# Down's first weight sums and slots placed anew, three pools of banks, and feed forward's first transposes ahead of the mixer's last row

## The chip, the cores and the metric

The kernel runs on one core of a Trainium2 chip. The metric is device time in microseconds. The engines are TensorE (PE; its weight loads are PEld), VectorE (DVE), ScalarE (ACT), GpSimd (POOL) and SyncE (SP), which issues the DMA transfers. Each engine works through its own list of instructions in order and waits on semaphores for the others.

## The reference

A block of two layers works on 1024 tokens of width 1024, in fp32. Layer 0's mixer joins a short convolution with attention over the 256 best keys; layer 1's is a gated delta rule. The two layers are:

```python
for i in range(2):
    hn = rmsnorm(h, norm_mix_g[i])
    h = h + (conv_dsa_mixer(hn, ...) if i == 0 else gated_deltanet_mixer(hn, ...))
    h = h + swiglu(rmsnorm(h, norm_ffn_g[i]), ffn_w_gate[i], ffn_w_up[i], ffn_w_down[i])
    e = rmsnorm(p[i] @ ple_w_proj[i], ple_post_norm_g[i])
    h = h + e * sigmoid(rmsnorm(h, ple_norm_g[i]) @ ple_w_gate[i])
```

The feed forward's width is 2816, and swiglu(n) is (silu(n @ w_gate) * (n @ w_up)) @ w_down.

## The kernel before

For l = 0 and 1 it runs mixer, feed forward (ffn), embedding stage (ple). A matrix operand in fp32 is split into a high and a low part (split: the high part is a copy on ACT, the low one a subtraction on DVE), and a product is three matmuls, high x high, high x low and low x high.

The feed forward multiplies 2 x 2 blocks with seven products instead of eight. So it needs sums of blocks: POOL makes those of the weights (wino: four sums of 128 x 512; S for gate/up, T_dn for down), those of the normed tokens (T1 to T4) and those of g (Sg). The blocks of tokens, B11, B21, B22 and T1 to T4, are transposed on TensorE (put, tp_f tiles) into H tiles. Gate/up (ffn_gu) goes through 22 groups of 128 hidden columns, two to a pair j: a group adds its seven products into three PSUM banks, pga, pgb and pgc, which ACT and DVE evacuate into g (gate) or u (up). After a pair, DVE multiplies u into g, POOL makes Sg, and SP stores both into a DRAM tile gfD.

Down (ffn_down) goes through 11 pairs in four units of 2, 3, 3 and 3 pairs, with seven steps in each. A step loads its block out of gfD into a slot (x), copies it (y on ACT), leaves the rest in x (DVE), splits its weights into the slot's other half (wh, wl), and multiplies into four banks, pda or pdb by turns; the banks are added into h. Slots are places in SBUF: pools s0 and s7, one tile s12 cut into pieces, and for step 3 the norm's buffers and s3. SBUF pools of the earlier stages are reused, so that a slot is free only when its former user is done.

Of the eight PSUM banks, gate/up uses pga 2, pgb/pgc 2 and the transposes 4, all in one pool, and down pda 4 and pdb 4, in one pool. The attention before has a pool of its own for mm (pswob) and one for its small tiles (tpy, y, tpp).

The order of the instructions comes from a scheduler that walks through the program with estimated times; self.after(marks) makes it issue what follows only after the instructions in marks. In layer 0 the attention's last row ends with finish (y is scaled into yR on DVE, transposed as tpy on TensorE, split, and multiplied by the output weights, pswob) and norm, and only then does the feed forward begin:

```python
            finish(*late)
            norm(NT - 1)
        self.gnes.close()
```

The feed forward's first group has the weights of group 0 behind the attention's last transposed probabilities:

```python
            with self.after(None if l else [self.last_pT]):
                w1, w2 = weights(0)
```

## Time and profile before

| | us |
|---|---|
| median of 3 runs | 2976.1 |
| lowest, highest | 2974.38, 2976.13 |
| profiled execution | 2976.15 |
| its span | 2974.3 |
| busy in it: PE, DVE, ACT, POOL | 2867.7, 1867.2, 1259.4, 1060.5 |

Times below are microseconds from the start of that span. Layer 0's mixer ends at about 689, its gate/up at 1130, its down at 1354; layer 1's mixer ends at 2206, its gate/up at 2650. In a row of the timeline stand the start, the length, the engine, the line, the operation with output and inputs, the shapes, the count, and in brackets the idle time before it and what ended it. Names are cut of their numbers. A row with a count covers several instructions and the gaps between them that the profile shows as none. In a row of waits stand the waiting and the awaited operation, the time in total, how often, and the longest.

### The profile page before, as it was taken

The numbers are of one execution on the slowest core, as the hardware profiler recorded it, in microseconds if no ns is written. First come the engines' busy times: TensorE is split into PE (matmuls) and PEld (weight loads), VectorE is DVE, ScalarE is ACT, GpSimd is POOL, SyncE is SP. The second block draws the span as 40 slices with busy tenths as digits, with TensorE's granted clock in tenths as the row PEclk, the third lists the DMA queues.
The fourth block names the chain that finished last, engine by engine and source line by source line (L and its number), as shares of the span: only waits on it lengthen the run. The fifth ranks groups of instructions, "written<-read, shape, count | busy, mean of one in ns | idle before, by whom it ended". The sixth has DMA issues, their size and how long they took to land.

```text
span 2974.3 us, 47842 instructions
## 1 busy us (share of the span) xinstructions
PE 2867.7 (96%) x19211; PEld 2388.5 (80%) x19211; DVE 1867.2 (63%) x3274; ACT 1259.4 (42%) x2226; POOL 1060.5 (36%) x931
## 2 busy tenths in 40 slices
PE   7999998999999998999999999999999999999999
PEld 6989876797888886888887777788678888878887
DVE  5799995455444448885466767664445444479871
ACT  4467725544333335434445455443233333344341
POOL 1341000114544436435212443342144455556333
PEclk9999998999999999999999999999999999999999
DMA  4122165201322225534332232223711322245422
GB/s 146 50 51 93 57 191 201 90 30 38 112 106 95 103 107 216 190 108 139 107 127 97 94 111 97 87 94 110 266 64 71 113 102 95 105 172 206 162 87 92
DMA packets 119822, 340.80 MB, mean 115 GB/s; under 512 B 11696, under 2 KB 34608, under 8 KB 101936
## 3 DMA queue, kind: packets, MB, share of 16 engines
q1 hardware_dynamic: 119600, 337.74, 32.9%
q8 instruction: 151, 2.47, 0.3%
q14 instruction: 71, 0.58, 0.1%
HBM read 240.64 MB, written 97.06 MB: 114 GB/s over the span
## 4 chain that ended last, share of the span: by engine, by line
PE 83%; DVE 8%; DMA 3%; ACT 3%; issue 2%; POOL 1%; SPq 0%; DVEq 0%; ACTq 0%; POOLq 0%
PE pga L852 16%; PE pgb L852 8%; PE pso L1369 7%; PE pdb L1027 6%; PE pda L1027 6%; PE psp L1138 6%; PE psz L216 4%; PE pgc L852 4%; PE pskqv L227 3%; PE psow L237 3%; PE psz L1629 2%; PE y L743 2%; PE pswob L237 2%; DVE sc L467 1%; PE tpp L734 1%
## 5 line engine op out<-in xcount | busy, mean ns | idle before, releaser
L1027 PE MATMUL pda<-sl 128*128 128x512 f32 x912 | 217.5, 396 | 12.4 <-DVE sl L109 12.3
L1027 PEld LDWEIGHTS pda<-sl 128*128 128x128 f32 x912 | 173.9, 191 | 51.7 <-DVE sl L109 15.4
L1027 PE MATMUL pdb<-sl 128*128 128x512 f32 x888 | 207.9, 391 | 5.4 <-DVE g L937 3.7
L782 POOL TENSOR_TENSOR S<-wr_gu 128x512 f32<-128x512 f32 x44 | 68.8, 1563 | 395.9 <-DMA wr_gu<-in_w_gu_dram 373.8
L1027 PEld LDWEIGHTS pdb<-sl 128*128 128x128 f32 x888 | 167.1, 189 | 41.9 <-DVE g L937 4.1
L109 DVE TENSOR_TENSOR w2l_gu<-S,w2h_gu 128x1024 fp32r<-128x1024 f32 x44 | 67.2, 1528 | 164.4 <-ACT w2h_gu L108 164.3
L1369 PE MATMUL pso<-hh,wl_od 128*128 128x512 f32 x384 | 157.3, 410 | 0.0
L1369 PE MATMUL pso<-hh,wh_od 128*128 128x512 f32 x384 | 156.9, 409 | 0.0
L1369 PE MATMUL pso<-hl,wh_od 128*128 128x512 f32 x384 | 156.4, 407 | 0.0
L1016 ACT CAST sl<-sl 128x1536 fp32r<-128x1536 f32 (+1 forms) x54 | 74.8, 1386 | 145.8 <-DMA sl<-gfD 143.1
L108 ACT CAST w2h_gu<-S 128x1024 fp32r<-128x1024 f32 x44 | 46.3, 1052 | 186.1 <-PE pga L852 94.1
L1387 DVE SCALAR_TENSOR_TENSOR c<-pso,odcw,c 128x509 f32<-128x509 f32 (+1 forms) x144 | 107.0, 743 | 26.5 <-ACT c L1384 24.9
L1017 DVE TENSOR_TENSOR sl<-sl 128x1536 fp32r<-128x1536 f32 (+1 forms) x54 | 103.3, 1914 | 24.7 <-ACT sl L1016 24.5
L227 PE MATMUL pskqv<-wh_kqv,hh 128*128 128x256 f32 x384 | 109.4, 285 | 0.3 <-ACT wh_kqv L108 0.3
L227 PE MATMUL pskqv<-wh_kqv,hl 128*128 128x256 f32 x384 | 108.7, 283 | 0.0
L227 PE MATMUL pskqv<-wl_kqv,hh 128*128 128x256 f32 x384 | 108.3, 283 | 0.0
L603 DVE TENSOR_SCALAR_CACHE_REDUCE tk_junk<-sc,tk_f 128x1024 int8<-128x1024 f32 (+5 forms) x111 | 102.5, 924 | 1.8
L153 POOL TENSOR_SCALAR nss_f<-nss_f 128x1 f32<-128x1 f32 x16 | 3.2, 200 | 273.2 <-ACT junk_f L152 273.2
L1138 PE MATMUL psp<-wh_pg,hh_p 128*128 128x512 f32 x256 | 100.5, 393 | 0.0
L1138 PE MATMUL psp<-wh_pg,hl_p 128*128 128x512 f32 x256 | 99.7, 390 | 0.0
L1138 PE MATMUL psp<-wl_pg,hh_p 128*128 128x512 f32 x256 | 99.7, 389 | 0.0
L600 ACT ACTIVATE tk_junka<-sc,tk_f 128x512 int8<-128x512 f32 (+2 forms) x93 | 83.7, 900 | 34.5 <-DVE tk_f L618 30.3
(543 smaller groups left out, 9013.3 us busy)
## 6 DMA issues: line engine op xcount, KB each, us to landing
wr_gu<-in_w_gu_dram SPq DMA_DIRECT2D x44, 1024.0 KB
sl<-gfD SPq DMA_DIRECT2D x42, 768.0 KB
gfD<-Sg SPq DMA_DIRECT2D x22, 1024.0 KB
wr_dn<-in_w_dn_dram SPq DMA_DIRECT2D x22, 1024.0 KB
wr_od<-in_w_qkv_dram SPq DMA_DIRECT2D x12, 1024.0 KB
...
```

What stands on the lines that cost most here:

```text
L216: nc.tensor.matmul(ps[:M, f * 512:(f + 1) * 512], a[:, kc, c], b[f][:, kc, :], start=(kc == 0 and i == 0), stop=(kc == KC - 1 and i == 2))
L227: nc.tensor.matmul(out, a[:, kc, c], b[:, kc, :], start=(kc == 0 and i == 0), stop=(kc == KC - 1 and i == 2))
L237: nc.tensor.matmul(ps[:, f * 512:(f + 1) * 512], a[:, kc, tsl], b[:, f * 512:(f + 1) * 512], start=(kc == 0 and i == 0), stop=(kc == nk - ...
L600: nc.scalar.activation(jk[:, :n], sc[b], AF.Sign, bias=fb, scale=-1.0, accum_out=c)
L603: v.tensor_scalar(jk[:, :n], sc[b], fb, 0.0, op0=op, op1=ALU.add, accum_out=c)
L852: nc.tensor.matmul(bank, a[:, kc, :], b[:, kc, :], start=first and kc == 0 and m == 0, stop=kc == 3 and m == 2, skip_group_check=True)
L1016: nc.scalar.copy(y, x.bitcast(F32))
L1017: v.tensor_tensor(x, x.bitcast(F32), y.bitcast(F32), op=ALU.subtract)
L1027: nc.tensor.matmul(ps, a[:, i, c], b[:, i, :], start=first and i == 0 and k == 0, stop=i == m - 1 and k == 2, skip_group_check=True)
L1138: nc.tensor.matmul(ps, a[:, kc, c], b, start=kc == 0 and i == 0, stop=kc == KC - 1 and i == 2)
L1369: nc.tensor.matmul(ps[:, f * 512:(f + 1) * 512], a[:, kc, :], b[f][:, kc, :], start=(kc == 0 and i == 0), stop=(kc == KC - 1 and i == 2))
L1387: nc.vector.scalar_tensor_tensor(c[:, e:(f + 1) * 512], ps[:, e - d:(f + 1) * 512 - d], cw[:, k:k + 1], c[:, e:(f + 1) * 512], op0=ALU.mul ...
```

## The change

1. A stage's banks lie in one pool for each tag (a, b, t) instead of one pool for all.
2. The last row's finish is cut in two. The scaling, tpy and the split stay where they are; pswob, the addition and the row norm (last_row) are issued in the feed forward's first group, behind the transposes of B11 and B21 in layer 0 and ahead of them in layer 1. Group 0's weights stand behind the last yR, and group 1's behind the last T sum.
3. The last pair's store to gfD is issued behind the loads of down's unit 0. T_dn of unit 1 stands behind the last Sg. The slots are cut anew, and a step's splits stand behind the splits of the step before and, from unit 1 on, behind the evacuation of three steps ago.
4. In the embedding stage the gate's first weights lie in four pools instead of one.

```diff
     def psum(self, es, name, **tags):
-        self.pss = self.pool(es, name, space=PSUM)
+        self.pss = {t: self.pool(es, name + t, space=PSUM) for t in tags}
...
     def tp(self, name, tag="tp"):
-        return self.pss.tile([P, 512], F32, tag=tag, bufs=self.tags[tag], name=name)
+        return self.pss[tag].tile([P, 512], F32, tag=tag, bufs=self.tags[tag], name=name)
...
                 ps = self.mm(f"pswob{i}")
-                self.mm_R2(ps, (yh, yl), slice(0, P), lambda k: [x[:, k % 2, :] for x in ws[k // 2]], 4)
-                row = self.row_home(i)
-                v.tensor_tensor(row, ps, row, op=ALU.add)
-                nc.sync.dma_start(self.hB[i * P:(i + 1) * P, :], row)
+                def out():
+                    self.mm_R2(ps, (yh, yl), slice(0, P), lambda k: [x[:, k % 2, :] for x in ws[k // 2]], 4)
+                    row = self.row_home(i)
+                    v.tensor_tensor(row, ps, row, op=ALU.add)
+                    nc.sync.dma_start(self.hB[i * P:(i + 1) * P, :], row)
+                return out
...
-            finish(*late)
-            norm(NT - 1)
-        self.gnes.close()
+            self.last_row = (finish(*late), junk(NT - 1))
...
         def group(n, x):
-            w1, w2 = weights(n)
+            with self.after([self.last_T] if n == 1 else None):
+                w1, w2 = weights(n)
...
         def first_group(x):
             hn = self.hn
-            with self.after(None if l else [self.last_pT]):
+            out, junk = self.last_row
+            with self.after(None if l else [self.last_yR]):
                 w1, w2 = weights(0)
+            def last_row():
+                out()
+                self.row_norm(NT - 1, junk)
+                self.gnes.close()
+            if l:
+                last_row()
...
             put("B21", lambda p: hn[2 * p][:, 512:])
+            if not l:
+                last_row()
...
-            nc.sync.dma_start(gD[j, :, 0:2, :], g[:, :, 0, :])
-            nc.sync.dma_start(gD[j, :, 2, :], g[:, 1, 1, :])
-            nc.sync.dma_start(gD[j, :, 3:7, :], S)
+            def store(j=j, g=g, S=S):
+                nc.sync.dma_start(gD[j, :, 0:2, :], g[:, :, 0, :])
+                nc.sync.dma_start(gD[j, :, 2, :], g[:, 1, 1, :])
+                nc.sync.dma_start(gD[j, :, 3:7, :], S)
+            if j < NFF // 2 - 1:
+                store()
+        return store
...
-        slots = itertools.chain((s0, 0, 2, None, 4, s0, 0), (s7, 3, s0, 0) * 3 + (s7, 3), (s0, 0, 3, s0, 0, 3, 0))
+        n0, n7, a, c = new(s0), new(s7), run(sa), cut((sb, 0, 0), (sb, 0, 1), (sa, 6144, None), (s3, 0, 0))
+        slots = itertools.chain((n0, a, run(sa, 4096), own, run(sb), n0, a), (c, n7, n0, a) * 3 + (c, n7), (n0, a, c, n0, a, n0, a))
...
-                self.wino(gp, [T[:, i] for i in range(4)], [q[:, i] for i in range(4)], "right")
+                with self.after([self.last_Sg] if ui == 1 else None):
+                    self.wino(gp, [T[:, i] for i in range(4)], [q[:, i] for i in range(4)], "right")
...
+                if (ui, si) == (0, 6):
+                    with self.after([get]):
+                        store()
...
-                with self.after([self.last_sum] if ui == 0 and si else None):
+                with self.after(prep + evac[:1] if ui else [self.last_sum] if si else None):
...
-            self.pad(es, 17, f"plp0{l}")
-            w0 = mk("w0")
+            self.pad(es, 1, f"plp0{l}")
+            w0 = [mk("w0a")]
+            self.pad(es, 16, f"plp1{l}")
+            w0 += [mk("w0b")] * 3
```

In the pieces below, names are cut of their layer and carry the buffer's number behind; where a line has moved, L852 is now L853, L885 is L896, L1027 is L1050 and L780 is L781. On TensorE, at layer 0's way into the feed forward, before:

```order
L681 MATMUL tpy_6461<-cf,yR_6457 128x128 x4
L237 MATMUL pswob_6468<-wh_wob_4566,yh_6459 128x512 x2
L237 MATMUL pswob_6468<-wl_wob_4567,yh_6459 128x512 x2
...
L237 MATMUL pswob_6468<-wh_wob_4587,yl_6460 128x512 x2
L885 MATMUL tp_f_B_6577<-cf,hn_f_0_4451 128x128 x4
L885 MATMUL tp_f_B_6584<-cf,hn_f_2_4453 128x128 x4
L885 MATMUL tp_f_B_6591<-cf,hn_f_4_4455 128x128 x4
L885 MATMUL tp_f_B_6598<-cf,hn_f_6_4457 128x128 x4
L885 MATMUL tp_f_B_6605<-cf,hn_f_0_4451 128x128 x4
L852 MATMUL pga_0_6574<-HB11h_6525,w1h_gu_0_6562 128x512
L885 MATMUL tp_f_B_6612<-cf,hn_f_2_4453 128x128 x4
```

Now:

```order
L681 MATMUL tpy_6468<-cf,yR_6464 128x128 x4
L237 MATMUL pswob_6475<-wh_wob_4573,yh_6466 128x512 x2
L237 MATMUL pswob_6475<-wl_wob_4574,yh_6466 128x512 x2
L896 MATMUL tp_f_B_6560<-cf,hn_f_0_4458 128x128 x4
L896 MATMUL tp_f_B_6567<-cf,hn_f_2_4460 128x128 x4
L896 MATMUL tp_f_B_6574<-cf,hn_f_4_4462 128x128 x4
L896 MATMUL tp_f_B_6581<-cf,hn_f_6_4464 128x128 x4
L237 MATMUL pswob_6475<-wh_wob_4573,yl_6467 128x512 x2
L237 MATMUL pswob_6475<-wh_wob_4573,yh_6466 128x512 x2
...
L237 MATMUL pswob_6475<-wh_wob_4594,yl_6467 128x512 x2
L896 MATMUL tp_f_B_6588<-cf,hn_f_0_4458 128x128 x4
...
L853 MATMUL pga_0_6557<-HB11h_6508,w1h_gu_0_6545 128x512
```

B11's transposes (four matmuls for each of hn 0, 2, 4 and 6) stand between the first four and the other twenty pswob matmuls, instead of behind the last one.

On TensorE at the step from gate/up to down, layer 0 (pga_21 is the last group's; a pd name goes on with the unit, the step that opened the bank, and the token block), before:

```order
L852 MATMUL pga_21_9313<-HT4l_6782,w2h_gu_21_9303 128x512
L852 MATMUL pga_21_9313<-HT4h_6781,w2l_gu_21_9304 128x512
L1027 MATMUL pda_0_0_0_9498<-sl_0_0_9490 128x512 x6
L1027 MATMUL pda_0_0_1_9506<-sl_0_0_9490 128x512 x6
L1027 MATMUL pda_0_0_2_9514<-sl_0_0_9490 128x512 x6
L1027 MATMUL pda_0_0_3_9522<-sl_0_0_9490 128x512 x6
L1027 MATMUL pdb_0_1_0_9486<-sl_0_9454 128x512 x6
L1027 MATMUL pdb_0_1_1_9487<-sl_0_9454 128x512 x6
L1027 MATMUL pdb_0_1_2_9488<-sl_0_9454 128x512 x6
L1027 MATMUL pdb_0_1_3_9489<-sl_0_9454 128x512 x6
L1027 MATMUL pda_0_0_0_9498<-sl_0_9454 128x512 x6
```

Now:

```order
L853 MATMUL pgb_21_9328<-HB22h_6522,w2l_gu_21_9318 128x512
L1050 MATMUL pdb_0_1_0_9507<-sl_0_9470 128x512
L1050 MATMUL pdb_0_1_1_9508<-sl_0_9470 128x512
L1050 MATMUL pdb_0_1_2_9509<-sl_0_9470 128x512
L1050 MATMUL pdb_0_1_3_9510<-sl_0_9470 128x512
L853 MATMUL pga_21_9327<-HT4h_6795,w2h_gu_21_9317 128x512
...
L853 MATMUL pga_21_9327<-HT4h_6795,w2l_gu_21_9318 128x512
L1050 MATMUL pdb_0_1_0_9507<-sl_0_9470 128x512
...
L1050 MATMUL pdb_0_1_3_9510<-sl_0_9470 128x512 x4
L1050 MATMUL pda_0_0_0_9519<-sl_0_0_9511 128x512 x6
L1050 MATMUL pda_0_0_1_9527<-sl_0_0_9511 128x512 x6
L1050 MATMUL pda_0_0_2_9535<-sl_0_0_9511 128x512 x6
```

Step 1 (pdb_0_1) has moved ahead of step 0 (pda_0_0), and its first four matmuls ahead of the last gate/up product.

On POOL at the same place, before:

```order
L780 TENSOR_TENSOR Sg_9_9169<-g_9_8937,Sg_9_9169 128x512
L780 TENSOR_TENSOR T_dn_0_9476<-wr_dn_0_9472 128x512 x2
L780 TENSOR_TENSOR T_dn_1_9481<-wr_dn_1_9474 128x512 x2
L780 TENSOR_TENSOR T_dn_0_9476<-wr_dn_0_9472,T_dn_0_9476 128x512
L780 TENSOR_TENSOR T_dn_1_9481<-wr_dn_1_9474,T_dn_1_9481 128x512
L780 TENSOR_TENSOR T_dn_0_9476<-wr_dn_0_9472,T_dn_0_9476 128x512
L780 TENSOR_TENSOR T_dn_2_9750<-wr_dn_2_9604 128x512 x2
L780 TENSOR_TENSOR T_dn_1_9481<-wr_dn_1_9474,T_dn_1_9481 128x512
L780 TENSOR_TENSOR T_dn_2_9750<-wr_dn_2_9604,T_dn_2_9750 128x512
L780 TENSOR_TENSOR T_dn_3_9755<-wr_dn_3_9606 128x512 x2
L782 TENSOR_TENSOR Sg_10_9409<-g_10_9177 128x512
L780 TENSOR_TENSOR Sg_10_9409<-g_10_9177 128x512
```

Now:

```order
L781 TENSOR_TENSOR Sg_9_9183<-g_9_8951,Sg_9_9183 128x512
L781 TENSOR_TENSOR T_dn_0_9497<-wr_dn_0_9493 128x512 x2
L781 TENSOR_TENSOR T_dn_0_9497<-wr_dn_0_9493,T_dn_0_9497 128x512 x2
L781 TENSOR_TENSOR T_dn_1_9502<-wr_dn_1_9495 128x512 x2
L781 TENSOR_TENSOR T_dn_1_9502<-wr_dn_1_9495,T_dn_1_9502 128x512 x2
L783 TENSOR_TENSOR Sg_10_9423<-g_10_9191 128x512
L781 TENSOR_TENSOR Sg_10_9423<-g_10_9191 128x512
L781 TENSOR_TENSOR Sg_10_9423<-Sg_10_9423,g_10_9191 128x512
L781 TENSOR_TENSOR Sg_10_9423<-g_10_9191,Sg_10_9423 128x512
L781 TENSOR_TENSOR T_dn_2_9773<-wr_dn_2_9624 128x512 x2
```

All sums of the first two pairs stand ahead of the last pair's Sg in both; the third and the fourth pair's have moved behind it, and the first pair's are no longer interleaved with the second's.

More of the change, by code (lines that the diff above doesn't have):

```diff
@@ L822, in ffn @@
         with ExitStack() as es:
-            self.ffn_down(es, l, gD)
+            self.ffn_down(es, l, gD, store)
         self.np2 = self.pool(self.hs, f"npool2{l}", side="right")
@@ L890, in sums @@
                 for p in range(NT // 2):
-                    f(T[:, p], *[hn[2 * p + o][:, k * 512:(k + 1) * 512] for k in range(2) for o in range(2)], p)
+                    self.last_T = f(T[:, p], *[hn[2 * p + o][:, k * 512:(k + 1) * 512] for k in range(2) for o in range(2)], p)
                 return T
@@ L953, in ffn_down, with own @@
             s0, ta, rw, tb = mk(0), mk(1), mk(2), mk(5)
-        s12 = mk(3).tile([P, 6 * 2048], F32R, name=f"sl12_{l}")
+        piece = lambda i, kb: mk(i).tile([P, kb * 256], F32R, name=f"sl{i}_{l}")
+        sa = piece(3, 32)
         self.pad(es, 1, f"ffp2{l}")
         tc_ = mk(6)
+        sb = piece(4, 16)
         s7 = mk(7)
         self.pad(es, 2, f"ffp3{l}")
-        s3 = mk(8)
-        slots = itertools.chain((s0, 0, 2, None, 4, s0, 0), (s7, 3, s0, 0) * 3 + (s7, 3), (s0, 0, 3, s0, 0, 3, 0))
+        s3 = piece(8, 8)
+        cut = lambda *at: lambda n, nm: [t[:, a if b is None else b * n:][:, :n] for t, a, b in at]
+        run = lambda t, a=0: lambda n, nm: [t[:, a + i * n:a + (i + 1) * n] for i in range(4)]
+        new = lambda p: lambda n, nm: run(p.tile([P, 6144], F32R, tag="slot", bufs=1, name=f"sl{nm}"))(n, nm)
+        def own(n, nm):
+            return [self.np.tile([P, D], F32R, tag="hn", bufs=2, name=f"sl{f}{nm}") for f in "xy"] + [s3[:, :n], s3[:, n:2 * n]]
+        n0, n7, a, c = new(s0), new(s7), run(sa), cut((sb, 0, 0), (sb, 0, 1), (sa, 6144, None), (s3, 0, 0))
+        slots = itertools.chain((n0, a, run(sa, 4096), own, run(sb), n0, a), (c, n7, n0, a) * 3 + (c, n7), (n0, a, c, n0, a, n0, a))
         ra, rb = (self.W, "wr", 2), (rw, "dr", 3)
@@ L1029, in ffn_down @@
                     if (hr, hc) in seen:
-                        v.tensor_tensor(hv, ps, hv, op=ALU.add)
+                        out = v.tensor_tensor(hv, ps, hv, op=ALU.add)
                     else:
-                        nc.scalar.copy(hv, ps)
+                        out = nc.scalar.copy(hv, ps)
+                evac = evac[-2:] + [out.ins]
                 seen.add((hr, hc))
```

61 lines of the change are left out of this document (26 added, 35 removed).

## The prediction

> **What bounds the kernel now.** I read the page first: busy shares and the chain of waits.
>
> ```profile
> PE 2867.7 (96%) x19211; PEld 2388.5 (80%) x19211; DVE 1867.2 (63%) x3274; ACT 1259.4 (42%) x2226; POOL 1060.5 (36%) x931
> PE 83%; DVE 8%; DMA 3%; ACT 3%; issue 2%; POOL 1%; SPq 0%; DVEq 0%; ACTq 0%; POOLq 0%
> ```
>
> TensorE is the bound, and the matmuls stay the same in number and shape. Only its idle time and its slow clock can be won, so I took the windows around the four kinds of places that the change touches (start:end, length, then busy time of each engine, PE's granted clock, DMA share, GB/s).
>
> ```profile
> 660.00:730.00 70.00, 62.88 (x363) 54.08 (x362) 41.73 (x57) 33.86 (x56) 32.34 (x26) 0.93 0.08 31
> 730.00:1125.00 395.00, 395.00 (x1727) 323.94 (x1727) 187.05 (x175) 132.61 (x180) 166.12 (x116) 1.00 0.30 107
> 1125.00:1200.00 75.00, 66.02 (x273) 52.61 (x272) 70.88 (x66) 36.61 (x55) 51.10 (x28) 0.91 0.56 199
> 1200.00:1335.00 135.00, 135.00 (x598) 111.81 (x597) 114.09 (x126) 46.57 (x57) 56.63 (x28) 1.00 0.45 157
> 1335.00:1390.00 55.00, 52.52 (x262) 43.60 (x261) 34.72 (x42) 31.23 (x49) 27.13 (x26) 1.00 0.32 111
> 2180.00:2270.00 90.00, 83.88 (x423) 69.74 (x422) 51.60 (x56) 34.14 (x58) 43.60 (x36) 0.98 0.12 44
> 2640.00:2720.00 80.00, 72.10 (x301) 57.53 (x300) 75.02 (x71) 39.56 (x60) 50.54 (x28) 0.94 0.59 211
> 2850.00:2910.00 60.00, 57.52 (x284) 47.73 (x284) 35.74 (x44) 31.83 (x50) 28.43 (x26) 1.00 0.28 92
> ```
>
> Between these places TensorE is never idle (395.00 of 395.00, 135.00 of 135.00). In them it is idle for 7.1, 9.0, 2.5, 6.1, 7.9 and 2.5 us, 35.1 in all. The clock under 1.00 adds, as an estimate, (1 - clock) times the length: 4.9 + 6.8 + 1.8 + 4.8 = 18.3 us. So the ceiling is about 53 us, 1.8% of the time. The waits in those windows say who is late (us in total, times, longest).
>
> ```profile
> PE tp_f_B L885 <- DVE HB11l L109: 3.4, 2, 2.0
> PE tpy L681 <- DVE yR L675: 2.7, 1, 2.7
> PE pda L1027 <- DVE sl L109: 4.9, 1, 4.9
> PE pdb L1027 <- DVE g L937: 3.7, 1, 3.7
> PE pda L1027 <- DVE sl L109: 7.4, 2, 6.3
> PE tp_f_T L885 <- DVE HT2l L109: 1.3, 1, 1.3
> PE tp_f_T L885 <- POOL T_f_T L830: 1.0, 1, 1.0
> PE tp_p L193 <- DVE hn_p L203: 1.9, 2, 1.3
> ```
>
> The first two are the way into layer 0's feed forward (A), the next two its step from gate/up to down (B0), the fifth the same step of layer 1 (B1), the sixth and seventh the way into layer 1's feed forward (C), the last the way into the embedding stage (D, once per layer).
>
> **A: into layer 0's feed forward.** The timeline there (start, length, engine, line, operands, count, idle before and its releaser):
>
> ```profile
> 675.56 2.03 DVE L109 TENSOR_TENSOR w1l_gu<-wr_gu,w1h_gu 128x1024 fp32r<-128x1024 f32 x1
> 677.52 1.74 DVE L109 TENSOR_TENSOR w2l_gu<-wr_gu,w2h_gu 128x512 fp32r<-128x512 f32 x1
> 679.19 0.68 DVE L675 TENSOR_TENSOR yR<-y,ri 128x512 f32<-128x512 f32 x1
> 679.92 1.11 PE L681 MATMUL tpy<-cf,yR 128*128 128x128 f32 x4 [2.71 <-DVE yR L675]
> 682.73 1.05 PE L237 MATMUL pswob<-wl_wob,yh 128*128 128x512 f32 x2
> 688.39 0.62 PE L237 MATMUL pswob<-wh_wob,yl 128*128 128x512 f32 x2
> 688.85 1.91 PE L885 MATMUL tp_f_B<-cf,hn_f 128*128 128x128 f32 x16
> 695.35 2.82 PE L885 MATMUL tp_f_B<-cf,hn_f 128*128 128x128 f32 x12 [1.41 <-DVE HB11l L109]
> ```
>
> Two weight differences stand on DVE ahead of yR, and TensorE waits 2.71 us for it. The change puts yR first: tpy starts at about 678.0 instead of 679.92, a gain of 1.9. The 16 transposes of B11 now stand behind the first four pswob matmuls, since the bank they write no longer belongs to the same pool as the pswob and y banks; their evacuations run while the remaining 20 pswob matmuls do, and B21's transposes find them done. That removes the two waits for HB11l, 3.4 in the row above. The 12 slow transposes (2.82 us, against 12/16 of 1.91 = 1.4 at speed) give 1.4 more. Against it, yl now stands behind both weight differences (2.03 + 1.74), and the pswob matmuls that read it may wait up to 0.7; I take 0.2. A = 1.9 + 3.4 + 1.4 - 0.2 = 6.5. From below 4.5, if the clock stays cold through B21 and yl costs the 0.7; from above 8, if part of the cold pswob rows (1.05 against 0.62) speeds up, too.
>
> **B: from gate/up to down.** TensorE, DVE and POOL in layer 0, then TensorE in layer 1:
>
> ```profile
> 1130.50 5.63 PE L1027 MATMUL pda<-sl 128*128 128x512 f32 x24
> 1135.96 4.24 PE L1027 MATMUL pdb<-sl 128*128 128x512 f32 x18
> 1143.89 2.93 PE L1027 MATMUL pdb<-sl 128*128 128x512 f32 x6 [3.68 <-DVE g L937]
> 1159.56 0.63 PE L1027 MATMUL pdb<-slw,sly 128*128 128x512 f32 x2
> 1126.89 0.69 DVE L869 TENSOR_TENSOR u<-pga,u 128x512 f32<-128x512 f32 x1
> 1127.50 3.44 DVE L109 TENSOR_TENSOR sl<-wr_dn,sl 128x512 fp32r<-128x512 f32 x2
> 1125.63 1.23 DVE L1017 TENSOR_TENSOR sl<-sl 128x1024 fp32r<-128x1024 f32 x1 [1.09 <-ACT sl L1016]
> 1133.10 2.31 DVE L1017 TENSOR_TENSOR sl<-sl 128x1024 fp32r<-128x1024 f32 x1
> 1127.40 6.92 POOL L780 TENSOR_TENSOR T_dn<-wr_dn 128x512 f32<-128x512 f32 x4 [28.80 <-PE pgb L852]
> 2650.03 1.09 PE L1027 MATMUL pda<-sl 128*128 128x512 f32 x4
> 2677.36 0.63 PE L1027 MATMUL pdb<-slw,sly 128*128 128x512 f32 x2
> ```
>
> From 1130.50 to the fourth step of unit 0 at 1159.56 are 29.1 us for 72 matmuls. The first 24 take from 1130.50 to 1135.96, 0.2275 each; at that speed 72 need 16.4. Lost: 12.7. In layer 1, 2677.36 - 2650.03 = 27.3, lost 10.9. The reason is one queue after another: POOL, idle for 28.80 us, begins the T_dn sums only after TensorE's last pgb; while POOL works, DVE's operations grow (1.23 to 2.31, 0.69 to 1.72); so g's evacuation, which frees a bank, and the weight differences out of T_dn come late.
>
> The change issues T_dn of the first pair as soon as its weights are there, 15 to 20 us earlier, inside POOL's idle time. It also lets down's step 1 go first, into the four transposing banks, which have long been free; four of its matmuls even precede the last gate/up product. Pda, which needs the banks that u and g leave, comes afterwards. What is left, for layer 0: step 1's second half needs three weight differences and one 1024-wide difference after u, at 0.69 to 1.72 and 1.23 to 2.31, middle 3 x 1.2 + 1.8 = 5.4, from 1127.5 to 1132.9. TensorE gets there at 1130.5, and 8 matmuls of step 1 that need none of this later, at 1132.3. I take 1.1 for that and its clock, and nothing for g's last product, which by the same durations (an estimate) is done a microsecond before pda's fourth bank. B0 = 12.7 - 1.1 = 11.6, bounds 6 (all of DVE's rows at their long values, g late, too) and 12.7.
>
> In layer 1 the new DVE order has the 1024-wide product of g (1.2 to 2.3 us) ahead of that difference and the last g behind all unit-0 splits, so I count 2.0 for the first wait, 2.3 for pda's fourth bank and 0.4 for the clock. B1 = 10.9 - 4.7 = 6.2, bounds 2 and 10.9.
>
> Then unit 1. Its first slot is free only when step 4 ends, 48 matmuls (10.9 us) ahead of its use. The load of such a slot:
>
> ```profile
> 1164.52 4.89 SPq L1011 DMA_DIRECT2D sl<-gfD  x2
> 1173.81 1.49 ACT L1016 CAST sl<-sl 128x1536 fp32r<-128x1536 f32 x1 [2.09 <-DMA sl<-gfD]
> 1175.60 1.74 DVE L1017 TENSOR_TENSOR sl<-sl 128x1536 fp32r<-128x1536 f32 x1
> ```
>
> The second load of the first row is issued as that row ends, at 1169.4, so 4.4 us pass to the copy, then 1.5 and 1.7: 8 us, plus whatever DVE has before it. Slack is about 2 us; I subtract 0.5 for each layer, 2 at most. Later units keep the rotation of four slots, whose waits TensorE didn't see (135.00 of 135.00).
>
> **C and D.** C: casts of B11 move ahead of the row norm's square on ACT, and two weight sums of the next group move behind the T sums on POOL. The waits of 1.0 and 1.3 should shrink to little, the one for HB11l by about half; 2.5 of 6.1, bounds -1 (S late for the second group) and 6. D: two of the four weight differences that POOL does beside DVE's last splits are done earlier, while the transposes still wait for h; 0.5 of 5.0 for both layers, bounds -2 and 3.
>
> **The sum.** 6.5 + 11.6 + 6.2 - 1.0 + 2.5 + 0.5 = 26.3. The profiled execution took 2976.15 (its span is 2974.3), the median of the runs is 2976.1, so the forecast is 2976.1 - 26.3 = 2950, its own range 2942 to 2958. Two edits are costed at nothing. The last pair's store now stands behind the loads of unit 0 on SP; only unit 3 reads it, two units of 7 x 8.2 us later (a step of three pairs has 36 matmuls of 0.2275), and without that cover B would wait for it. The second group's weight sums stand behind the T sums on POOL in layer 0, too; the first group's products cover that by some 2 us, and without it TensorE would wait for two sums of up to 1.7 (the POOL row above has this form).
>
> **A rule on the clock.** After 2.71 us of idleness (row of tpy) the pswob pairs take 1.05 instead of 0.62. The Trainium skill, page "TensorE: Matmul & The Clock Gate", Part 1, has the clock halve after an idle window of about 3.4 us. The trace differs, since that gap is shorter. By the rule no wait that I leave (2.3 at most) would cost any clock, and the sum would be about 1 larger.
>
> **Rivals.** (1) DVE takes TensorE's place at B. It is busy for 70.88 of 75.00 and 75.02 of 80.00 there, and 114.09 of 135.00 after; the stretch is to lose 12 us. For it: the order is full of splits that precede evacuations. Against it: much of the 70.88 is the stretching beside POOL, and POOL's 8 sums partly move ahead. Then B0 gives 6 and B1 3: 6.5 + 6 + 3 - 1 + 2 + 0.5 = 17, 2959. (2) Nearly everything is won: no wait at B, and the clock stays up; 8 + 12.7 + 10.9 + 5 + 2 = 38.6, 2938. (3) It doesn't do what it says at B, because the pools land on the same banks or DVE's queue still ends late: A and C alone, 8 to 9, 2967. (4) Slower. Splits of units 1 to 3 now follow the split before and the evacuation three steps back. If such a split stands in DVE's queue for its load, the h additions behind it hold the banks, and TensorE waits once in each of 21 steps, in both layers. From 26/42 = 0.6 us for each this eats the gain; at 0.8 it is 34 against 26, 2984. For it: DVE at 85% and ACT waiting for loads (2.09 in the row above). Against it: three steps ahead are 3 x 8.2 = 24 us, and a load with its splits needs 8 plus DVE's backlog.
>
> **Numbers.** Forecast 0.50, (1) 0.22, (2) 0.12, (3) 0.08, (4) 0.07, no change at all 0.01. Less than 0.2% (6 us) can't be told from no change here. Faster by more: all but (4), the last, and a part of (3): 0.89; within 0.2%: 0.04; slower 0.07. The range 2937 to 2965 holds the forecast, (1) and most of (2), 0.82.
>
> **What would show it.** Right: POOL's T_dn rows start near 1105 in layer 0; from the last pga to slot step 3 about 18 us; tpy's wait under 1 us and none for HB11l in layer 0; windows between the places still fully busy. Wrong: a wait of 3 us or more of pda or pdb for DVE; B21 still slow; short waits of pd rows spread over units 1 to 3.

## The result and the profile after

The changed kernel takes 2960.1 us (median of 4 runs, 2958.5 to 2964.3); the kernel before took 2976.1 beside it. The ratio is 0.9948, with a 95% interval of 0.9931 to 0.9965: faster by 16.0 us. The forecast was 2950, its range 2937 to 2965. The profiled execution took 2959.12, its span is 2957.3.

The page of the changed kernel (busy times, then shares of the chain of waits) differs little from that of before:

```profile
PE 2858.4 (97%) x19211; PEld 2381.3 (81%) x19211; DVE 1873.6 (63%) x3274; ACT 1254.8 (42%) x2226; POOL 1026.3 (35%) x931
PE 82%; DVE 8%; DMA 3%; ACT 3%; issue 2%; POOL 2%; SPq 0%; DVEq 0%; ACTq 0%; POOLq 0%
```

The windows at the places of the prediction, of the changed kernel (columns as there):

```profile
660.00:723.50 63.50, 54.62 (x333) 47.21 (x333) 46.18 (x53) 30.96 (x52) 30.04 (x26) 0.95 0.09 34
723.50:1118.00 394.50, 394.50 (x1726) 323.59 (x1725) 185.57 (x175) 131.65 (x179) 168.94 (x120) 1.00 0.29 102
1118.00:1193.00 75.00, 73.02 (x318) 59.11 (x317) 62.92 (x71) 39.37 (x58) 42.46 (x25) 1.00 0.62 224
1193.00:1328.00 135.00, 135.00 (x597) 111.85 (x596) 123.77 (x128) 49.62 (x63) 63.30 (x31) 1.00 0.48 171
2185.00:2260.00 75.00, 65.95 (x333) 54.00 (x332) 47.23 (x47) 28.84 (x48) 37.31 (x30) 0.95 0.11 39
2630.00:2710.00 80.00, 77.00 (x328) 61.89 (x327) 63.57 (x71) 41.30 (x63) 41.95 (x25) 0.98 0.59 210
```

At the step to down (third and sixth row) TensorE idles for 2.0 and 3.0 us where it idled for 9.0 and 7.9, at clocks of 1.00 and 0.98 instead of 0.91 and 0.94. At the ways into the feed forwards (first and fifth) it still idles for 8.9 and 9.1. The waits tell why. Of the changed kernel, the longest over the whole span, then those from 1100 to 1200, from 2630 to 2720, and at the way into the embedding stage:

```profile
PE pga L853 <- DVE w1l_gu L109: 14.3, 2, 7.1
...
PE pdb L1050 <- DVE sl L1040: 2.0, 2, 1.4
...
PE pdb L1050 <- DVE sl L109: 2.1, 1, 2.1
...
PE tp_p L193 <- DVE hn_p L203: 1.9, 2, 1.3
```

The first is new, once in each layer. It stands where gate/up's second group (group 1) begins, behind one single DVE operation. The timeline of the changed kernel there, layer 0 and then layer 1:

```profile
675.01 0.66 PE L681 MATMUL tpy<-cf,yR 128*128 128x128 f32 x4 [0.78 <-DVE yR L675]
683.69 1.91 PE L896 MATMUL tp_f_B<-cf,hn_f 128*128 128x128 f32 x16
...
693.01 5.11 POOL L831 TENSOR_TENSOR T_f_T<-hn_f 128x512 f32<-128x512 f32 x4 [0.91 <-PE tp_f_T L896]
698.08 1.29 POOL L783 TENSOR_TENSOR S<-wr_gu 128x512 f32<-128x512 f32 x1
699.32 1.31 POOL L781 TENSOR_TENSOR S<-wr_gu 128x512 f32<-128x512 f32 x1
700.58 1.31 POOL L783 TENSOR_TENSOR S<-wr_gu 128x512 f32<-128x512 f32 x1
701.83 1.29 POOL L781 TENSOR_TENSOR S<-wr_gu 128x512 f32<-128x512 f32 x1
698.65 2.48 DVE L109 TENSOR_TENSOR HB22l<-tp_f_B,HB22h 128x512 fp32r<-128x512 f32 x4 [2.05 <-ACT HB22h L108]
702.95 11.12 DVE L109 TENSOR_TENSOR w1l_gu<-wr_gu,w1h_gu 128x1024 fp32r<-128x1024 f32 x1 [1.81 <-ACT w1h_gu L108]
703.07 5.04 POOL L831 TENSOR_TENSOR T_f_T<-hn_f,T_f_T 128x512 f32<-128x512 f32 x4
708.06 2.48 POOL L781 TENSOR_TENSOR S<-S,wr_gu 128x512 f32<-128x512 f32 x2
710.50 2.48 POOL L781 TENSOR_TENSOR S<-wr_gu,S 128x512 f32<-128x512 f32 x2
714.12 0.80 PE L853 MATMUL pga<-HB11h,w1l_gu 128*128 128x512 f32 x1 [7.12 <-DVE w1l_gu L109]
...
2216.29 11.18 DVE L109 TENSOR_TENSOR w1l_gu<-wr_gu,w1h_gu 128x1024 fp32r<-128x1024 f32 x1 [1.77 <-PE tp_f_T L896]
2227.52 0.79 PE L853 MATMUL pga<-HB11h,w1l_gu 128*128 128x512 f32 x1 [7.14 <-DVE w1l_gu L109]
```

The operation w1l is a subtraction of 1024 columns. In the row of the kernel before that follows further down its neighbour takes 2.31 us beside POOL, and the same form takes about 1.2 alone (the row at 1125.63 in the prediction). Here it takes 11.12 and 11.18. It reads the raw weights and w1h, so it doesn't wait for any of POOL's sums as data. But it ends 1.1 us after POOL's run of sums does (712.98 and 714.07), and POOL's run has no break from 693.01 on. TensorE waits for 7.1 us, and the next matmuls (from 714.72 on) take 0.63 each; one at speed takes 0.39 (the row at 1128.09 further down). It is the slow clock again: from 712.3 to 719.1 the granted clock is 0.50.

To see where the time went, I cut both profiled executions into places, from the starts of TensorE's rows: the lead (up to the last row of attention, where TensorE begins to wait for yR), A (from there to the last gate/up product of layer 0), B0 (from there to the first tp_p), layer 1's mixer, C (first tp_f_B to the last gate/up product of layer 1), B1 and the tail behind the second tp_p. Down products issued ahead of the last gate/up product are counted to B, at 0.2275 us each. Gains against the kernel before, in us:

| kernel | lead | A | B0 | mixer 1 | C | B1 | tail | sum |
|---|---|---|---|---|---|---|---|---|
| predicted | | 6.5 | 11.1 | | 2.5 | 5.7 | 0.5 | 26.3 |
| changed | 3.0 | 0.1 | 11.0 | -0.3 | -3.8 | 7.0 | 0.0 | 17.0 |
| no rule for group 1 | -4.2 | 7.0 | 12.4 | 1.2 | -0.6 | 8.1 | -1.6 | 22.2 |
| rule on group 2 | 0.9 | 4.8 | 12.3 | 1.1 | -1.7 | 7.9 | -0.2 | 25.0 |
| entry as before | -0.2 | 3.4 | 12.0 | 0.2 | -1.6 | 6.7 | -1.6 | 18.9 |
| chained sums | -0.9 | 8.5 | 12.1 | 3.1 | 5.0 | 6.2 | 0.0 | 34.0 |
| break ahead of the request | 3.2 | 9.1 | 6.5 | -0.9 | 5.5 | 8.0 | 0.0 | 31.3 |
| one pool | 1.2 | -6.1 | 13.6 | -0.9 | -5.3 | 9.7 | -1.8 | 10.5 |
| down as before | 0.6 | -0.1 | 1.6 | -0.9 | -4.3 | -3.1 | -0.9 | -7.0 |
| no rule for Sg | -1.6 | -1.2 | 4.0 | -2.4 | -5.3 | 2.2 | -1.6 | -5.9 |
| late sums | 3.1 | -3.3 | 4.8 | -5.1 | -3.8 | 3.8 | 0.0 | -0.4 |
| best | 0.0 | 8.9 | 11.8 | 2.7 | 4.4 | 8.8 | -0.2 | 36.4 |

The predicted 0.5 for unit 1's first slot is taken off B0 and B1. The lead and mixer 1 hold the same instructions in all these kernels, and yet they vary by 7.4 and 8.2 us between the profiled executions. So sums of one execution can be off by several us, and verdicts on a cause rest on the places. The places come from one execution each, too. In the five kernels from "changed" to "chained sums", whose down is written alike, B0 lies between 11.0 and 12.4 and B1 between 6.2 and 8.1, so a difference of 2 us at a place says little by itself.

### The profile page after: what moved, and what is told of

It is laid out like the page before. It is cut to its first block, busy times and chain, and to the rows that moved or that the text cites. A ratio compares the mean times of both kernels' runs of the same rounds, so it can differ in the third digit from the quotient of the medians.

```text
span 2957.3 us, 47840 instructions
## 1 busy us (share of the span) xinstructions
PE 2858.4 (97%) x19211; PEld 2381.3 (81%) x19211; DVE 1873.6 (63%) x3274; ACT 1254.8 (42%) x2226; POOL 1026.3 (35%) x931
## 4 chain that ended last, share of the span: by engine, by line
PE 82%; DVE 8%; DMA 3%; ACT 3%; issue 2%; POOL 2%; SPq 0%; DVEq 0%; ACTq 0%; POOLq 0%
PE pga L853 16%; PE pgb L853 8%; PE pdb L1050 7%; PE pso L1395 7%; PE pda L1050 7%; PE psp L1164 6%; PE psz L216 4%; PE pgc L853 4%; PE psow L237 3%; PE psz L1655 2%; PE pskqv L227 2%; PE y L746 2%; DVE sc L467 1%; PE pswob L237 1%; DMA dupk<-kD 1%
## 5 line engine op out<-in xcount | busy, mean ns | idle before, releaser
L1050 PE MATMUL pda<-sl 128*128 128x512 f32 x912 | 212.2, 390 | 0.5 <-ACT h L1055 0.5
L1050 PEld LDWEIGHTS pda<-sl 128*128 128x128 f32 x912 | 171.1, 188 | 36.8 <-ACT h L1055 1.3
L109 DVE TENSOR_TENSOR w2l_gu<-S,w2h_gu 128x1024 fp32r<-128x1024 f32 x44 | 74.4, 1690 | 174.6 <-ACT w2h_gu L108 174.6
L1050 PE MATMUL pdb<-sl 128*128 128x512 f32 x528 | 124.8, 394 | 2.7 <-DVE sl L109 2.1
L1413 DVE SCALAR_TENSOR_TENSOR c<-pso,odcw,c 128x509 f32<-128x509 f32 (+1 forms) x144 | 107.1, 744 | 26.3 <-ACT c L1410 24.6
L1050 PEld LDWEIGHTS pdb<-sl 128*128 128x128 f32 x528 | 100.1, 190 | 24.9 <-DVE sl L109 2.6
L1040 DVE TENSOR_TENSOR sl<-sl 128x1536 fp32r<-128x1536 f32 (+1 forms) x54 | 106.3, 1968 | 13.6 <-ACT sl L1039 13.2
```

What stands on the lines that cost most here:

```text
L1040: v.tensor_tensor(x, x.bitcast(F32), y.bitcast(F32), op=ALU.subtract)
L1050: nc.tensor.matmul(ps, a[:, i, c], b[:, i, :], start=first and i == 0 and k == 0, stop=i == m - 1 and k == 2, skip_group_check=True)
L1413: nc.vector.scalar_tensor_tensor(c[:, e:(f + 1) * 512], ps[:, e - d:(f + 1) * 512 - d], cw[:, k:k + 1], c[:, e:(f + 1) * 512], op0=ALU.mul ...
```

## The experiments

The theory after the result: DVE's w1l is kept out by POOL's unbroken run of sums, which the rule "group 1's weights behind the last T sum" has made longer. The rivals: the sums come too late as data, the entry with B11's transposes in front is at fault, or it is the pools. In the diffs, a minus is a line of the changed kernel.

### The rule for group 1 taken away

```diff
-            with self.after([self.last_T] if n == 1 else None):
-                w1, w2 = weights(n)
+            w1, w2 = weights(n)
```

> Group 1's weights no longer stand behind the last T sum, so POOL makes the S sums of groups 1 and 2 before or among the T sums and its run beside the long weight difference (w1l of group 1, 11.1 us in both layers) gets shorter. Theory H (while POOL works without a pause, this difference gets nothing): w1l falls below 5 us in layer 0 and TensorE's wait for it from 7.1 to under 2; T1 and T2 come up to 3 us later, so that a wait of 1 to 3 us for T may appear; time about 2952. Rival F (the difference is long by itself, by its operands or their place): w1l stays at 11 us, the waits stay at 7.1, and the time stays at 2960.

Measured: 2949.6 us (2946.5 to 2953.9), ratio 0.9913 (0.9898 to 0.9928), so 10.5 faster than the changed kernel. Its w1l rows and its waits at the way into layer 1's feed forward:

```profile
712.81 2.74 DVE L109 TENSOR_TENSOR w1l_gu<-wr_gu,w1h_gu 128x1024 fp32r<-128x1024 f32 x1 [1.80 <-ACT w1h_gu L108]
2219.74 3.70 DVE L109 TENSOR_TENSOR w1l_gu<-wr_gu,w1h_gu 128x1024 fp32r<-128x1024 f32 x1 [1.79 <-PE tp_f_T L895]
PE tp_f_T L895 <- POOL T_f_T L831: 5.0, 1, 5.0
```

The wait for w1l is gone. In layer 1 the transposes now wait 5.0 for a T sum, which stands behind group 1's sums again. So the rule does something for T, and loses more than that on DVE. Here, too, w1l ends 1.1 us after a break or the end of POOL's run; only this comes one or two sums after the one that was under way at the request, and not eight.

### Group 1's sums made three times

```diff
-            self.wino(gp, [S[:, i] for i in range(4)], [q[:, i] for i in range(4)], "left")
+            for _ in range(3 if n == 1 else 1):
+                self.wino(gp, [S[:, i] for i in range(4)], [q[:, i] for i in range(4)], "left")
```

> POOL makes the S sums of group 1 three times instead of once (same values), that is 8 more sums of 1.24 us in the same run in both layers. Theory H: w1l grows from 11.1 by up to 9.9 us to about 21, its end stays about 1.1 us behind the end of POOL's run, and TensorE waits about 17 us for it instead of 7.1, so the time is about 2980. Rival F: w1l stays at 11 us; TensorE waits for the S sums instead. Rival G (it gets its turn where a sum on POOL waits for POOL's own earlier result): w1l ends at the first such place, 11 us or less.

Measured: one run of 2982.2 us. The longest wait, w1l and the POOL row at which it ends:

```profile
PE pga L854 <- DVE w1l_gu L109: 24.0, 2, 12.0
707.84 16.00 DVE L109 TENSOR_TENSOR w1l_gu<-wr_gu,w1h_gu 128x1024 fp32r<-128x1024 f32 x1 [1.81 <-ACT w1h_gu L108]
721.49 1.26 POOL L781 TENSOR_TENSOR S<-S,wr_gu 128x512 f32<-128x512 f32 x1
722.83 2.15 POOL L781 TENSOR_TENSOR S<-wr_gu,S 128x512 f32<-128x512 f32 x1
```

The longer run holds w1l longer, 16.0 us, and both waits grow by 4.9. But it doesn't hold it to the run's end. Between 722.75, where the row at 721.49 ends, and 722.83 POOL has a break of 0.08 us: that sum reads the one just before it. There DVE gets its turn, 1.0 us before w1l ends at 723.84.

### The rule on group 2 instead of group 1

```diff
-            with self.after([self.last_T] if n == 1 else None):
+            with self.after([self.last_T] if n == 2 else None):
```

> Group 1's S sums stand ahead of T1, group 2's behind the T sums, so POOL's run beside w1l is four sums (5.0 us) shorter. Theory H: w1l lasts 6 us instead of 11.1, TensorE's wait in layer 0 falls from 7.1 to 2.1, in layer 1 to 2 or 3 with up to 1.5 more for T1; time about 2951. Rival F: 11 us and 7.1 us as before, time 2960.

Measured: 2951.0 us (2945.7 to 2953.1), ratio 0.9913 (0.9896 to 0.9929). Here w1l takes 5.05 and 5.14, TensorE waits 0.6 and 0.7 for it, and 5.0 for a T sum in layer 1.

```profile
2215.65 5.14 DVE L109 TENSOR_TENSOR w1l_gu<-wr_gu,w1h_gu 128x1024 fp32r<-128x1024 f32 x1 [1.76 <-PE tp_f_T L896]
```

It is as fast as without the rule. In both layers w1l ends 1.1 us after a break of 0.08 us (at 712.11 and 2219.71), three sums after the one that was under way at the request; so less of a run behind the request costs less.

### The entry into the feed forward as before

```diff
-            with self.after(None if l else [self.last_yR]):
+            out()
+            self.row_norm(NT - 1, junk)
+            self.gnes.close()
+            with self.after(None if l else [self.last_pT]):
...
-            if not l:
-                last_row()
```

The rule for group 1 is taken away here, too.

> The way into the feed forward as in the kernel before (last row and row norm first, group 0's weights behind the last transposed probabilities, no edge for group 1); pools, down and the embedding stage as changed. Both theories: the step to down keeps its gains of 11.0 and 7.0 us, the waits for HB11l (3.4 and 2.0) and yR (2.7) are back, no w1l wait over 2 us. If the new entry's gain was eaten in full by the w1l wait, layer 0 stands as with the change (within 1 us) and layer 1 is 3.8 us better: time 2956. If the three separate pools alone made the 3.0 us that appeared within the attention, they stay; if they were chance, the time may be up to 2959.

Measured: 2953.9 us (2950.2 to 2958.3), ratio 0.9927 (0.9911 to 0.9943). Against the kernel without the rule, this differs by the entry alone: 4.3 us of the medians, and 3.6 at A (7.0 and 3.4). The intervals overlap, so the entry's worth of some 4 us rests on the place A and on its waits:

```profile
PE tpy L681 <- DVE yR L675: 2.7, 1, 2.7
PE tp_f_B L890 <- DVE HB11l L109: 0.6, 2, 0.4
```

The 2.7 for yR is back. The waits for HB11l, which were expected back as well, aren't: 0.6 instead of the 3.4 of before, although the transposes stand behind the last row.

### Group 1's and 2's sums chained

```diff
+            if n in (1, 2):
+                do = {0: (S[:, 0], q[:, 2], q[:, 3], ALU.add), 1: (S[:, 1], S[:, 0], q[:, 0], ALU.subtract),
+                      2: (S[:, 2], q[:, 0], q[:, 2], ALU.subtract), 3: (S[:, 3], q[:, 1], S[:, 1], ALU.subtract)}
+                for i in (0, 1, 3, 2):
+                    with self.after([self.last_T]):
+                        self.last_T = gp.tensor_tensor(*do[i][:3], op=do[i][3]).ins
...
-                sub(T2[:, p], hn[2 * p][:, 512:], T2[:, p])
+                self.last_T = sub(T2[:, p], hn[2 * p][:, 512:], T2[:, p])
```

> Groups 1 and 2 of gate/up: POOL makes the four weight sums of a group one behind the other, behind the last T sum, in the order sum 0, sum 1 (reads sum 0), sum 3 (reads sum 1), sum 2. No work is added or left out. POOL's run of sums is as long as in the changed kernel (16 sums from 693 to 713 in layer 0), but its first sum that reads the sum just before it now ends its wait at about 704.4. Theory (DVE's w1l difference gets its turn at the first sum of POOL that waits for POOL's own sum before it): w1l takes about 2.5 us in each layer instead of 11.1, TensorE has no wait for w1l, and the time is 2960 - 7.1 - 7.1 = 2946. Rival (DVE is held until POOL's whole run ends): w1l takes about 10 us in each layer, TensorE waits about 6 us twice, 2958.

Measured: 2944.5 us (2942.2 to 2950.9), ratio 0.9899 (0.9879 to 0.9918), 15.6 faster than the changed kernel, against 14 expected. POOL's run and w1l:

```profile
703.44 5.08 POOL L831 TENSOR_TENSOR T_f_T<-hn_f,T_f_T 128x512 f32<-128x512 f32 x4
708.27 2.57 DVE L109 TENSOR_TENSOR w1l_gu<-wr_gu,w1h_gu 128x1024 fp32r<-128x1024 f32 x1 [1.81 <-ACT w1h_gu L108]
708.47 1.29 POOL L844 TENSOR_TENSOR S<-wr_gu 128x512 f32<-128x512 f32 x1
709.84 2.16 POOL L844 TENSOR_TENSOR S<-S,wr_gu 128x512 f32<-128x512 f32 x1
```

POOL does the same sums, and w1l takes 2.57 (2.65 in layer 1). It begins to work at the break between 709.76 and 709.84, and POOL's next sum takes 2.16 instead of 1.29, since now POOL waits. No wait of TensorE for w1l is left. Of the 15.6 us, 10.5 came with the rule's removal alone; the other 5.1 lie within overlapping intervals, and at the places they are 1.5 at A, 5.6 at C and 1.9 in mixer 1.

### The same sums in the order 0, 2, 1, 3

```diff
-                for i in (0, 1, 3, 2):
+                for i in (0, 2, 1, 3):
```

(The minus is a line of the kernel with the chained sums.)

> The same kernel as the one with the chained sums, but a group's sums in the order 0, 2, 1, 3, so that only sum 3 reads the sum just before it. Nothing else differs. Theory (first sum that waits for the one before it): that sum comes two sums of 1.25 us later, so w1l takes about 5.0 us in each layer, TensorE waits about 1 us in each, time about 2948. Rival (until the run ends): w1l takes about 10 us as with the other order, 2958. A third reading (any sum that reads a POOL result, however old, lets DVE in): 3.7 us.

Measured: one run of 2946.5 us. The row of w1l in layer 0:

```profile
706.93 5.05 DVE L109 TENSOR_TENSOR w1l_gu<-wr_gu,w1h_gu 128x1024 fp32r<-128x1024 f32 x1 [1.81 <-ACT w1h_gu L108]
```

5.05 as expected (5.0), 5.09 in layer 1, and TensorE waits for it for 1.1 in each. The first break moved by two sums, and w1l's end with it. That the run must end (10 expected), or that any sum which reads an older one is enough (3.7 expected), are both out.

### A break ahead of the request

```diff
+            early[1] = chain(1, (0, 1, 3, 2))
             for p in range(NT // 2):
-                sub(T2[:, p], hn[2 * p][:, 512:], T2[:, p])
+                with self.after([self.last_T]):
+                    self.last_T = sub(T2[:, p], hn[2 * p][:, 512:], T2[:, p])
```

Here chain makes a group's four sums as above; group 2's are made in the order 0, 2, 1, 3.

> Group 1's four weight sums stand chained (each reads the one before it: 0, 1, 3, then 2) between T3's and T4's sums on POOL, so the breaks in POOL's run come at about 699 to 701 in layer 0, ahead of the moment (about 703) at which DVE asks for w1l. From then on eleven... the four T4 sums and group 2's sums 0, 2, 1 follow without a break, some 9 us, until group 2's sum 3 waits for sum 1 at about 712. Nothing is left out. Theory by order (DVE gets its turn only at the first sum that waits for the one just before it, after its request): w1l takes 9 to 10 us, TensorE waits 5 to 7 us for it in each layer, about 2958. Theory by length (only a run that has gone on for about seven sums or 9 us without a break at the request keeps DVE out; over the traces so far no request after six sums or fewer was held): at the request POOL's run is two to three sums old, DVE gets in at the next end of a sum, w1l takes 1.3 to 2.6 us, TensorE has no wait for it, about 2945.

Measured: 2948.8 us (2944.9 to 2951.8), ratio 0.9908 (0.9893 to 0.9922).

```profile
699.24 1.30 POOL L843 TENSOR_TENSOR S<-S,wr_gu 128x512 f32<-128x512 f32 x1
700.63 1.28 POOL L843 TENSOR_TENSOR S<-wr_gu,S 128x512 f32<-128x512 f32 x1
701.87 1.28 POOL L843 TENSOR_TENSOR S<-wr_gu 128x512 f32<-128x512 f32 x1
702.73 1.50 DVE L109 TENSOR_TENSOR w1l_gu<-wr_gu,w1h_gu 128x1024 fp32r<-128x1024 f32 x1 [1.81 <-ACT w1h_gu L108]
703.11 7.07 POOL L831 TENSOR_TENSOR T_f_T<-hn_f,T_f_T 128x512 f32<-128x512 f32 x4
```

The breaks stand ahead of these two chained sums, at 699.2 and 700.6, before DVE asks at 702.73, and the next one comes at 713.94. Still w1l takes 1.50 (1.59 in layer 1) and goes in at the next end of a sum, at 703.15. So the theory by order is only half of it: a break also counts when it lies shortly before the request. What holds DVE out is a run that is already long when it asks. A gains 9.1 and C 5.5, the most of all kernels. The time is no better than with the chained sums because at B0 it loses 5.6 against them, to a wait of 4.0 for a weight difference. Down's code wasn't touched; the scheduler put DVE's work there in another order, so that two differences out of T_dn (2.86 from 1120.92 on) stand beside POOL's sums. An edit can move instructions far from its own place.

### One pool for a stage's banks

```diff
-        self.pss = {t: self.pool(es, name + t, space=PSUM) for t in tags}
+        self.pss = self.pool(es, name, space=PSUM)
...
-        return self.pss[tag].tile([P, 512], F32, tag=tag, bufs=self.tags[tag], name=name)
+        return self.pss.tile([P, 512], F32, tag=tag, bufs=self.tags[tag], name=name)
```

> The changed kernel with a stage's banks in one pool again, the rest as changed. By the order of the instructions, layer 0's first four transposes then stand behind the last pswob product as before the change, and down's first products are pda's again. Theory (the pools carry the way into layer 0's feed forward and a part of the step to down): the waits for HB11l of 3.4 us come back, and in down pda waits for the banks that u and g leave, 2 to 5 us in each layer: about 2960 + 3.4 + 7 = 2970. Rival (the pools move instructions but no time, since the wait for w1l and the placing of down's sums decide): 2960, with w1l still at 11 us. A second rival: all of the gain at the step to down comes from the pools, 2960 + 18 = 2978.

Measured: 2965.8 us (2962.4 to 2968.0), ratio 0.9964 (0.9952 to 0.9976), 5.6 slower than the changed kernel. At A it loses 6.2 and at C 1.5 against that, although TensorE waits 4.8 for w1l there and not 7.1: in layer 0 it has waits of 2.5 for HB11l again, and in layer 1 of 2.0. At B it gains 2.6 and 2.7, where the first theory expected a loss. So the pools help the way into the feed forward. At the step to down no gain of theirs is seen, and whether they cost something there isn't shown: with the sums chained, one pool in down gives -0.3 and +2.6 (the last experiment).

### Down as before

The function for down is that of before, and the last pair's store stands ahead of the loads.

> The changed kernel with the whole of down as before the change (slots, order of the weight sums, the last pair's store ahead of the loads), the rest as changed, three pools too. Theory (the gain at the step to down comes from the slots and from POOL's early sums): POOL's first T_dn sum starts at about 1127 again, pdb or pda waits 3 to 5 us for DVE in each layer, the 18 us gained at that step are lost again, 2960 + 18 = 2978. Rival (the gain comes from the three pools, which let pdb's banks be written ahead of gate/up's last product): the time stays at 2960, and the kernel with one pool loses the 18.

Measured: 2986.3 us (2983.2 to 2993.7), ratio 1.0038 (1.0022 to 1.0054): slower than the kernel before. The step to down loses 9.4 and 10.2 us against the changed kernel, 19.6 where 18 were expected; the rival's pools aren't it. POOL's T_dn begins at 1127.43 again, and TensorE waits:

```profile
1127.43 6.91 POOL L781 TENSOR_TENSOR T_dn<-wr_dn 128x512 f32<-128x512 f32 x4 [28.80 <-PE pgb L853]
PE pda L1045 <- DVE sl L109: 3.7, 1, 3.7
PE pdb L1045 <- DVE sl L1035: 3.5, 1, 3.5
```

The other parts of the change (pools, entry, embedding stage) lose about 10 us by the medians, when they stand alone: by the places, A wins nothing, C loses 4.3 to the hold of w1l, and B1 loses 3.1.

### Late T_dn sums with the new slots

```diff
+                if not ui:
+                    for i in (0, 2):
+                        gp.tensor_scalar(T[:, i, 0:1], self.last_x[:, 1, 1, 0:1], 1.0, 0.0, op0=ALU.mult, op1=ALU.add)
                 with self.after([self.last_Sg] if ui == 1 else None):
```

> The changed kernel with its slots, but POOL's T_dn sums of down's unit 0 wait for gate/up's last evacuation out of pga (four tiny POOL operations read it first), so that they start at about 1125 in layer 0 as before the change, interleaved, and not at 1103. Theory (POOL's early start is what wins at the step to down): TensorE waits for DVE's differences out of T_dn again, 6 to 10 us in each layer, 2960 + 16 = 2976. Rival (the slots and the order of the steps win it): under 4 us in both layers, 2962.

Measured: one run of 2976.5 us. The sums begin at 1131.73, the step to down loses 6.2 and 3.3 us against the changed kernel, 9.5 instead of the 16 expected; the total agrees with the 2976 expected by luck, since the rest lies in A and mixer 1, which the edit doesn't touch. In layer 0 TensorE's waits aren't the expected ones either: 2.0 for a weight difference, and 3.7 for ACT's copies of the banks into h. The four tiny operations take 3.4 us themselves, so that the sums begin 4 us later than before the change. So POOL's early start seems worth half of the 18 us there at most, by one execution.

### Unit 1's sums free of the rule for Sg

```diff
-                with self.after([self.last_Sg] if ui == 1 else None):
-                    self.wino(gp, [T[:, i] for i in range(4)], [q[:, i] for i in range(4)], "right")
+                self.wino(gp, [T[:, i] for i in range(4)], [q[:, i] for i in range(4)], "right")
```

> The changed kernel without the rule that puts unit 1's T_dn sums behind the last Sg: POOL makes all sums of the third pair and some of the fourth's ahead of Sg. Theory (POOL beside DVE's splits costs DVE its pace at the step to down): sums beside the splits from 1125 on stretch them, 2 to 5 us more in each layer, about 2966. Rival (only the first pairs' early sums count): within 1 us in each layer, 2960.

Measured: one run of 2982.0 us; 7.0 and 4.8 us lost at the step to down, where 2 to 5 were expected. In layer 0 it is one wait for the last product of g:

```profile
PE pda L1049 <- DVE g L950: 6.0, 1, 6.0
```

The prediction put g's last product at nothing in layer 0, and had no term for the rule that keeps POOL off it. Without the rule the third pair's sums stand beside DVE's splits and make g's evacuation late: three differences out of T_dn ahead of it take 5.12 us, in the changed kernel 1.88.

### Chained sums and one pool in down

```diff
-        self.psum(es, f"ffpd{l}", a=4, b=4)
+        self.psum(es, f"ffpd{l}", a=4, b=4, one=True)
```

Added to the kernel with the chained sums; with one=True all tags share one pool.

> The kernel with the chained sums (order 0, 1, 3, 2 behind T4), and for down alone the banks in one pool, so that down's step 0 (pda) goes first as in the kernel with one pool everywhere, where the time from the last gate/up product to the embedding stage was 209.5 and 212.6 us, against 210.1 and 215.2 with three pools and chained sums. Theory (pda first is a little better once POOL's sums are early): about 3 us less than with the chained sums alone, 2941. Rival (the two orders are equal, and the difference was jitter or the cost of the first four early products, 0.9 us each layer): 2944.

Measured: 2940.4 us (2938.1 to 2941.1), ratio 0.9879 (0.9862 to 0.9895). It is the fastest kernel here, 35.8 us ahead of before and 19.8 ahead of the changed one. Over the chained sums alone it has 4.2 us of the medians, within overlapping intervals; at B the places give -0.3 and +2.6. So whether the order with pda first is any better stays open.

## Why the prediction was right, and where it was wrong

The direction held, and so did the range of 2937 to 2965. The time came out 10 us above the forecast, outside the narrower 2942 to 2958 that the sum gave, and its parts stand apart from the total.

- **What bounds the kernel** was read rightly. Between the places TensorE is fully busy as before (394.50 of 394.50, 135.00 of 135.00), and all the gain lies in its waits and clock.
- **B0 and B1** were right: 11.0 and 7.0 us against 11.1 and 5.7 (with the slot's 0.5 off each). POOL's first sums start early, at 1103.09 and 1105.59 as foreseen:

```profile
1103.09 2.54 POOL L781 TENSOR_TENSOR T_dn<-wr_dn 128x512 f32<-128x512 f32 x2 [7.29 <-DVE w1l_gu L109]
1105.59 2.67 POOL L781 TENSOR_TENSOR T_dn<-wr_dn,T_dn 128x512 f32<-128x512 f32 x2
1128.09 0.39 PE L853 MATMUL pga<-HT4h,w2l_gu 128*128 128x512 f32 x1
1130.01 3.91 PE L1050 MATMUL pdb<-sl 128*128 128x512 f32 x16 [0.60 <-DVE sl L1040]
1141.92 0.63 PE L1050 MATMUL pdb<-sl,sly 128*128 128x512 f32 x2
```

  Step 3 begins 13.6 us behind the last gate/up product, not 18, because its first matmuls went ahead of the rest of step 2. The reasons were right in kind: late sums cost 9.5 of the 18 us, and down as before costs all of it. But I named only two, the early sums and the order of the steps. The third, unit 1's sums behind Sg, costs 11.8 when it alone is left out, and I had no term for it. These don't add up to 18; that each takes away the cover of the others is my reading, and no run shows it. Unit 1's first slot costs 1.36 in layer 0 (the 2.0 in two waits above has 0.60 and this), 0.5 foreseen. In layer 1 the first wait is 2.1 (2.0 foreseen), those of pda and behind it 0.9 (2.3 foreseen), and the clock costs more than the 0.4: it is 0.50 from 2644.2 to 2647.6, and the twenty matmuls behind the wait take 6.46 where twenty at 0.2275 take 4.6.
- **A and C** are the error: 0.1 and -3.8 against 6.5 and 2.5, each below its own bound of 4.5 and -1. The steps named for them happened. The wait for yR is 0.78, none is left for HB11l in layer 0, and the transposes of B21 run at speed (1.91 for 16). With the hold of w1l away, the kernel with the chained sums has 8.5 and 5.0 there, more than foreseen. The step that failed is the edit that was costed at nothing: "The second group's weight sums stand behind the T sums on POOL in layer 0, too; the first group's products cover that by some 2 us, and without it TensorE would wait for two sums of up to 1.7". I asked when POOL's sums would be ready as data, and not what POOL's longer run does to the DVE operation beside it, one that needs none of these sums. It measured 7.1 us in each layer, and with the slow clock behind it up to 8.4 and 8.9 (what the chained sums gain over the changed kernel at A and C). All the signs named for "right" came and none of those for "wrong"; none of them looked at a wait of gate/up's banks.
- **A sign of it stood in the profile before**, and the prediction doesn't use it. In layer 1 the kernel before has the same operation at 6.32, and a wait of TensorE behind it:

```profile
2233.42 6.32 DVE L109 TENSOR_TENSOR w1l_gu<-wr_gu,w1h_gu 128x1024 fp32r<-128x1024 f32 x1 [1.77 <-ACT w1h_gu L108]
2239.66 2.31 DVE L109 TENSOR_TENSOR w1l_gu<-S,w1h_gu 128x1024 fp32r<-128x1024 f32 x1
PE pga L852 <- DVE w1l_gu L109: 1.8, 1, 1.8
```

  A row of five times its usual length, where the other subtractions of this size in the feed forwards are at most about twice as long (2.35), is worth a question of its own.
- **The clock.** The prediction has the slow pswob pairs follow from 2.71 us of idleness, less than the rule that it cites. The length of that gap doesn't decide: in the kernel with one pool the same pairs take 1.05 behind waits of 0.79 and 0.68 alone, in the changed kernel 0.63 behind 0.78 and 0.68. What does decide stays open.
- **D** is nothing instead of 0.5. The wait for hn_p is 1.9 in two parts in both kernels.
- **The rivals.** The time is that of rival (1), 2959, but by luck and not by its way: DVE at the step to down is busy for 62.92 of 75 us, less than before, and no wait there exceeds 2.1. Rival (2) had the sizes of B0 and B1 too high; its A and C of 8 and 5 are what the kernel with chained sums shows. Rival (3) is refuted by B, and rival (4) by the full windows of units 1 to 3.
- **What the total hides.** Of the 17.0 us between the two profiled executions, 3.0 lie in the lead, which the change doesn't touch. The places that it touches give 14.3, against 26.3 foreseen: A and C fall short by 12.7, D by 0.5, and B0 and B1 are 1.2 over. That the range held with two of its four parts outside their bounds is owed to its width.
